# Start addresses of operand parts: split activations and weights placed 0 to 240 bytes into larger tiles

## The chip, the cores and the metric

One core of a Trainium2 chip runs one program. The metric is device time in microseconds of one execution; the median of three runs stands for a kernel.

## The reference

Two stacked blocks on 256 tokens of width 1024, batch 1, in float32. The first block has two layers, each with a gated feed forward, an attention of three kinds of heads (block-sparse, indexed top-64, stick-breaking) and a second gated feed forward, all with a modulated norm. The second block has four layers, each with a mixer (state space, gated linear attention, gated delta rule, state space), attention to a memory of 256 tokens, and a feed forward with a short convolution. Nearly all of the arithmetic is products of activations with weights:

```python
def swiglu(h, w1, w3, w2):                      # first block: 1024 -> 2816 -> 1024, four times
    return (jax.nn.silu(h @ w1) * (h @ w3)) @ w2

def conv_glu_ffn(h, up_w, conv_w, conv_b, down_w):   # second block, four times
    gate, up = jnp.split(h @ up_w, 2, axis=-1)
    gate = causal_dwconv(gate, conv_w) + conv_b
    return (jax.nn.silu(gate) * up) @ down_w
...
        x = x + mix                              # mixer: projections of rmsnorm(x), and an output product
        x = x + memory_cross_attention(rmsnorm_2(x, ln_xattn[i]), rmsnorm_2(mem, ln_mem[i]), ...)
        x = x + conv_glu_ffn(rmsnorm_2(x, ln_ffn[i]), ...)
```

## The kernel before, in words

Activations lie with channels on the 128 partitions and the 256 tokens along them. Every float32 operand of a large product is an exact sum of two parts, a high part (`h` at the end of its name) that ScalarE writes as a copy and a low part (`l`) that another engine writes as the rest (`split`, lines 244 to 247). A product is three matmuls in float32r, high x high, high x low and low x high (`mm3`, line 297), each with a weight load of its own of 128 x 128 and 256 columns of the moving operand; all are issued on line 283.

Weights come from memory in slabs of one MB, 128 partitions x 2048 values (`slab`, line 249): a DMA fills `w` (three places), ScalarE writes `wh`, VectorE `wl` (three places each); with `share` set GpSimd writes a piece of `wl`. An up slab holds 8 chunks of the contraction by 256 columns: one slab is 2 x 8 x 3 = 48 matmuls. A down slab holds 2 chunks by 1024 columns: 48 matmuls too.

Which operand is moving and which the weights: in most products slabs are the weights and the activation moves. In products that leave tokens on the partitions (`proj_half`, `wide_half`) chunks of the activation are the weights and the slab moves. In the profile a matmul is named out<-moving,weights: `up<-hl,wh` moves `hl` over weights from `wh`.

Activation parts: `hh`, `hl` of a norm's output, [128, 8, 256], one place each, made in `norm` (line 550) and `norm_shift` (line 556); `norm_shift` also makes `eh`, `el`, [128, 8, 258], used by the first two slabs of a stage of the first block; `gh`, `gl`, [128, 512], two places each, made in `glu` (line 664) for the input of the down products; `mh`, `ml` of the memory; `oh`, `xoh`, `myh`, `hyh`, `gyh` and their low parts before output products.

`glu` runs over 11 steps of 256 of the 2816 inner columns. A step is two up slabs (96 matmuls) and, one step behind, one down slab (48 matmuls); both blocks use it. The instructions of TensorE stand in the order of the trace within a chain; otherwise a scheduler keeps the order of the program. `gdn_combine` (from line 1888) inverts 128 x 128 triangular matrices of the delta rule, four at a time, and holds a 64 x 64 corner of four of them in `q2` (four places).

Tiles are packed one behind the other along each partition, on multiples of 32 bytes: constants, then `w`, then `wh` and `wl`, then the pool of the norms (`hh`, `hl` and what belongs to them), then what the stage at hand needs. First bytes within a partition in the program before, and what is left of them modulo 256:

| parts | first byte | modulo 256 |
|---|---|---|
| `wh`, three places | 64544, 72736, 80928 | 32 |
| `wl`, three places | 89120, 97312, 105504 | 32 |
| `hh`, `hl` | 120896, 129088 | 64 |
| `eh`, `el` (rows of 1032 bytes) | 212832, 221088 | 96, 160 in the first row, 8 more in each next |
| `gh`, `gl` in the first block | 159968 (and places behind it) | 224 |
| `gh`, `gl` in the second block | 157760 (and places behind it) | 64 |
| `mh`, `ml` in the first stage | 153792, 170176 | 192 |
| `myh`, `hyh`, `xoh`, `xqh`, `xkh`, `xvh` and their low parts | | 64 |
| `oh`, `gyh` and their low parts | | 0 |

Within a tile all of these step by 512 or 1024 bytes from one matmul's operand to the next, but for `eh`, `el`, and but for slabs of the indexer (`wide_half`), whose moving rows are 264 or 320 values long.

Of the kernel before, what the change touches and what calls it, by code (L numbers as in the profile page):

```python
# [9 lines left out]
F32R = mybir.dt.float32r  # L10
# [6 lines left out]
P = 128  # L17
T = 256
# [8 lines left out]
# ---------------------------------------------------------------- layout of small vectors  # L27
# [17 lines left out]
def _consts():  # L45
# [11 lines left out]
        # sums from after a chunk's middle to each token, or negative from after the token to the middle  # L57
# [12 lines left out]
def _prepare(i):  # L70
    """Lays the inputs out: weights as slabs in the order they are used, vectors as columns."""
# [15 lines left out]
    def up(w, order=None):  # L87
        """[.., 1024, n] -> [.., n / 256, 128, 8, 256], column blocks of 128 in the order given."""
        lead, n = w.shape[:-2], w.shape[-1]
        w = w.reshape(-1, KC, P, n // P, P)  # L90
        if order is not None:
            w = w[:, :, :, order]
        nb = w.shape[3]
        w = w.reshape(-1, KC, P, nb // 2, 2 * P).transpose(0, 3, 2, 1, 4)
        return np.ascontiguousarray(w).reshape(*lead, nb // 2, P, KC * 2 * P)

    def down(w):
        """[.., k, 1024] -> [.., k / 256, 128, 2, 1024]."""
        lead, k = w.shape[:-2], w.shape[-2]
        w = w.reshape(-1, k // 256, 2, P, D).transpose(0, 1, 3, 2, 4)  # L100
        return np.ascontiguousarray(w).reshape(*lead, k // 256, P, 2 * D)

    def wide(w):
        """[.., 1024, n] -> [.., 2, 128, 4, n]: halves of the contraction."""
# [4 lines left out]
    def flat(w):  # L109
        """[.., 1024, n] -> [.., 128, 8 * n]."""  # L110
# [62 lines left out]
# ---------------------------------------------------------------- the program  # L173


class Normed:
    """The parts of something to be normed, and each token's factor, once it is worked out."""
# [10 lines left out]
class Net:  # L188
    def __init__(self, tc, a, out):
# [16 lines left out]
        self.n = 0  # L206

    # ---- small helpers

    @contextmanager  # L210
    def phase(self, name):
        """Tiles of a part of the program, given back at its end."""
# [31 lines left out]
    def split(self, src, hi, lo, engine=None):  # L244
        """src as a sum of two parts; returns the two instructions."""
        a = self.nc.scalar.activation(hi, src, AF.Copy)  # L246
        return a, (engine or self.nc.vector).tensor_tensor(lo, src, hi.bitcast(F32), op=OP.subtract)  # L247

    def slab(self, src, n=2048):
        """A slab of weights, as two parts that add up to it exactly."""  # L250
# [6 lines left out]
        hi = self.t([P, 2048], "wh", F32R, pool=self.sp)[:, :n]  # L257
        lo = self.t([P, 2048], "wl", F32R, pool=self.sp)[:, :n]
        m = n // self.pieces
        for k in range(0, n, m):  # L260
# [6 lines left out]
            if self.slabs == 2:  # L267
                # this slab's place is in use until the norm's input is there
                for x, y in zip(s, self.normed):
                    self.after(x, y)  # L270
# [14 lines left out]
    def link(self, ins):  # L285
        """In a chain the tensor engine keeps to the order that is traced."""
# [10 lines left out]
    def mm3(self, out, a, b, start, stop):  # L297
        """out += a.T @ b, both given as exact sums of two parts."""
# [7 lines left out]
    def rsqrt(self, out, src, scale):  # L306
        """out = (src * scale + eps) ** -0.5"""
# [3 lines left out]
    def newton(self, r, src, scale, n):  # L311
        """One step of Newton's for r = (src * scale + eps) ** -0.5"""
# [8 lines left out]
    def after(self, ins, before):  # L321
        """Issues ins behind an earlier instruction of its engine."""
# [7 lines left out]
    def act(self, out, src, func, **k):  # L330
        """An activation of one of the two tables in use: Silu's, or the one with both Ln and Exp. The scalar
        engine takes turns with them as they are traced."""
# [11 lines left out]
    # ---- start  # L344

    def load_cols(self):
        """All vectors but the memory's gains."""
# [33 lines left out]
    def load_consts(self):  # L381
        """Tables, and masks made from them."""
# [11 lines left out]
        # biases: queries on partitions (keys after the query), keys on partitions (keys from the query on)  # L394
# [9 lines left out]
    def start(self, kv):  # L404
        """The first of the memory's keys and values go along with the first modulation."""
# [17 lines left out]
    # ---- modulation  # L423

    def ada_slab(self, l, s):
        """256 columns of layer l's modulation: rows of its weights, over partitions, with silu(c)."""
# [30 lines left out]
    def need(self, l, chunk):  # L457
        """Has columns [chunk * 1024, ..) of layer l's modulation worked out by now."""
# [3 lines left out]
    def mod_cols(self, l, i):  # L462
        """(gain, shift) of the i-th norm of layer l."""
# [19 lines left out]
    # ---- norms  # L483

    def square_sums(self, b, x, s, engine=None, behind=None):
        """Adds the squares of x's pair of chunks b to the sums so far; the last give what is left to add up."""
# [29 lines left out]
    def rstd(self, parts, cols=False, r=None):  # L516
        """Each token's reciprocal root mean square, on all partitions; with cols also over tokens, behind."""
# [12 lines left out]
    def parts_of(self, x, gain, eh, el, sums=True, beside=None):  # L530
        """The parts of x * gain; and the sums of x's squares, but for the last addition."""
# [18 lines left out]
    def norm(self, gain, cols=False):  # L550
        """x normed, as the parts of x * gain, and a factor for each token, which goes to what comes of
        products with them."""
        e = [self.t([P, KC, T], "h" + k, F32R, pool=self.hp) for k in "hl"]
        return Normed(self, e, self.parts_of(self.x, gain, *e), cols)

    def norm_shift(self, gain, shift):
        """x normed and shifted: h, its parts; and for products that need not wait for the root mean
        square: e, x normed, with the parts of the shift behind each chunk."""
# [7 lines left out]
        h = [self.t([P, KC, T], "h" + k, F32R, pool=self.hp) for k in "hl"]  # L566
# [23 lines left out]
    def scale(self, out, ps, r):  # L590
        """out [128, n, T] = products with e, of a bank or a part of it, times r."""
# [5 lines left out]
    def project(self, src, n, tag, bufs=2, bank=None):  # L597
        """Two blocks of a projection of x normed: [128, 2, T]."""
# [7 lines left out]
    # ---- feed forward  # L606
# [5 lines left out]
    def down_step(self, acc, w, j, g, first, last, banks=range(4)):  # L612
        """acc += w[k-chunk j].T @ g"""
# [4 lines left out]
    def down_pair(self, acc, w, g, first, last):  # L618
        """acc += w.T @ g; in the last step one bank after the other is done."""
# [9 lines left out]
    def up_pair(self, out, w, n):  # L629
        """out[j] = w[block j].T @ n; with the first of a norm's products the high parts come first, and then  # L630
        the root mean square. Blocks in halves of a bank, or in two."""
# [32 lines left out]
    def glu(self, part, down, side):  # L664
        """down.T @ part(s, out), in four banks; part works out two blocks of rows at a time."""
# [7 lines left out]
        for s in range(ns):  # L673
            g = self.t([P, 2, T], "g")
            part(s, g)
            gs = [self.t([P, 512], "g" + x, F32R) for x in "hl"]
# [48 lines left out]
    # ---- first block's attention  # L725
# [4 lines left out]
    def proj_tokens_from(self, src, n, h):  # L730
        """h.T @ w for n columns: two banks, tokens on partitions."""
# [5 lines left out]
    def wide_half(self, ps, src, n, h, q):  # L737
        """One half of the contraction of h.T @ w."""
# [8 lines left out]
    def rotate(self, q, t=None):  # L747
        """Rotary embedding of the first 16 dims of each head, in place; q: [128, heads, 64] of one half of
        the tokens, or [128, 2, heads, 64]."""
# [13 lines left out]
    def tok_halves(self, l, n, h, out):  # L763
        """256 columns of a projection, over tokens, in two steps: out [128, 2, 256]."""
# [7 lines left out]
    def qk_halves(self, l, n, k, h, dst):  # L772
        """Norm, gain, rotation and, in a third step, transposition of four heads of queries or keys:
        dst [128, 2, T], queries scaled."""
# [23 lines left out]
    def index_halves(self, l, h, d):  # L798
        """The indexer's projections, in four steps; then their transposition, in two."""
# [35 lines left out]
    def select(self, d):  # L835
        """A bias for each query and key: 0 where the key is among the query's best 64, else -1e30. Five steps
        for the scores, six for the best."""
# [39 lines left out]
    def softmax_head(self, qk, j, v, out, bias=None):  # L877
        """One head, in three steps: qk [128, 4, T] (query pairs, scaled, and key pairs), v [128, 2, 64] tokens,
        out [64, T] in PSUM."""
# [34 lines left out]
    def stick_head(self, q, k, v, out, bank):  # L914
        """Stick-breaking, in three steps: q, k [64, T] (q scaled), v [128, 2, 64] tokens; keys on partitions."""
# [25 lines left out]
    def head_pair(self, head, l, p, oh, ol, wait):  # L941
        """Two heads, one a step behind the other, in four steps; in a fifth the norm of each, gain, and its
        parts."""
# [35 lines left out]
    def attention(self, l):  # L979
        nc, a = self.nc, self.a  # L980
        h, e = self.norm_shift(*self.mod_cols(l, 1))
        # queries and keys of the first stick-breaking heads
# [16 lines left out]
    def qkc_halves(self, l, p, h, q):  # L999
        """Queries and keys of two stick-breaking heads, in two steps: q [128, 2, T]."""  # L1000
# [9 lines left out]
    def attention_heads(self, l, h, qkc):  # L1010
        """Half a slab at a time, with a step of what goes on beside it behind."""
# [78 lines left out]
    # ---- second block: memory attention  # L1090
# [11 lines left out]
    def mem_first(self):  # L1102
        """The memory, and the first slab by turns with it: and what works out the slab's parts, piece by piece."""
        m = self.t([P, KC, T], "mem", bufs=1)
        w = self.t([P, 2048], "w", pool=self.wp)
        self.ready = hi, lo = [self.t([P, 2048], "w" + k, F32R, pool=self.sp) for k in "hl"]
# [6 lines left out]
    def kv(self, i, m=None):  # L1113
        """Keys and values of layer i's memory attention, in steps of a slab."""
# [23 lines left out]
    def proj_pair(self, ps, w, h):  # L1138
        """h.T @ w for 256 columns: the two halves of the tokens in the halves of a bank."""
# [11 lines left out]
    def cross(self, i):  # L1151
# [9 lines left out]
        with self.chained():  # L1161
# [6 lines left out]
            # each head goes through: queries (two steps), scores, turned probabilities, output  # L1168
# [24 lines left out]
    def cross_head(self, hd, kT, v, n, src, oh, ol):  # L1193
        """One head of memory attention, in five steps."""
# [61 lines left out]
    # ---- second block: state space mixer  # L1256

    def softplus(self, out, v, bias, n, tag):
        """out = softplus(v + bias); v, out [n, T]"""
# [8 lines left out]
    def mamba(self, i):  # L1268
        """Half a slab at a time, with what follows on it in between."""
# [3 lines left out]
            "dt": self.t([P, 2, 64], "mdk", bufs=1),  # dt of all heads, and log decays, over tokens  # L1273
# [33 lines left out]
    def mamba_steps(self, ia, n, d):  # L1307
        """dt for all heads, and the log decays' sums: from each token to the end of the first
        half (negative), or from the start of the second."""
# [33 lines left out]
    def out_proj(self, w, gh, gl, n, gate=None):  # L1343
        """x += (w.T @ (gh + gl)) * gate, from 2 * n blocks of rows."""
# [775 lines left out]
```

## Time and profile before

| | |
|---|---|
| runs | 3250.59, 3248.66, 3244.77 us, median 3248.66 |
| span of the profiled execution, first to last instruction | 3242.8 us |
| TensorE matmuls | 25,866, busy 3123.4 us |
| VectorE busy | 2406.3 us |
| ScalarE busy | 1874.0 us |
| GpSimd busy | 614.6 us |
| mean granted clock of TensorE | 0.989 of 2.4 GHz |
| moved by DMA | 624.85 MB, mean 193 GB/s |

The median of the runs is 5.9 us over the span of the profiled execution: the span begins with the first instruction and ends with the last. Busy times of matmuls overlap, since they are pipelined; the time that one matmul takes of TensorE's stream is read from the starts of successive ones, not from its duration.

### The profile page before, as it was taken

The page shows a single profiled execution, that of the slowest core. Times are in us where ns is not written, and L with a number is a line of the kernel's source. Part 1 is how long each engine was busy: PE and PEld are TensorE (multiplying, and loading weights), DVE is VectorE, ACT ScalarE, POOL GpSimd, SP SyncE. Part 2 cuts the span into 40 slices and gives each one's busy share as a digit, 9 for nine tenths or more (in the row PEclk, how much of TensorE's full clock was granted, in tenths as well). Part 3 has the DMA queues.
Part 4 walks back from the last instruction along what each step waited for, and adds up shares of the span by engine and source line. Part 5 has one row for each costly group of instructions (what it writes and reads, how often), then busy time and mean ns, then how long its engine had stood idle before and what let it go on. Part 6 is the DMA issues. An engine that isn't in the chain of part 4 may idle for free. (4 is left out here: it accounts for less than half of the span.)

```text
span 3242.8 us, 63167 instructions
## 1 busy us (share of the span) xinstructions
PE 3123.4 (96%) x25866; PEld 3022.4 (93%) x25866; DVE 2406.3 (74%) x4122; ACT 1874.0 (58%) x3317; POOL 614.6 (19%) x522
## 2 busy tenths in 40 slices
PE   8999999999999999999999999998899999999998
PEld 8999889999988999889999999997799999889998
DVE  6877778777776857887767677688857766887765
ACT  5544566454466546775546655476466545776544
POOL 1100232010032102433001220036422000443100
PEclk9999999999999999999999999999999999999999
DMA  8978436758843655444554445544334555545453
GB/s 286 320 292 312 175 125 216 292 216 298 303 171 120 220 185 187 164 163 170 182 186 155 142 169 173 191 163 157 130 118 156 198 196 186 176 163 184 162 188 118
DMA packets 96754, 624.85 MB, mean 193 GB/s; under 512 B 10640, under 2 KB 14800, under 8 KB 25424
## 3 DMA queue, kind: packets, MB, share of 16 engines
q1 hardware_dynamic: 96464, 620.82, 54.7%
q8 instruction: 203, 3.33, 0.4%
q14 instruction: 87, 0.71, 0.1%
HBM read 607.08 MB, written 13.70 MB: 191 GB/s over the span
## 5 line engine op out<-in xcount | busy, mean ns | idle before, releaser
L246 ACT ACTIVATE wh<-w 128x512 fp32r<-128x512 f32 (+3 forms) x1392 | 1034.7, 788 | 773.7 <-issue 251.0
L247 DVE TENSOR_TENSOR wl<-w,wh 128x512 fp32r<-128x512 f32 (+3 forms) x1195 | 1140.9, 982 | 370.9 <-ACT wh L246 367.3
L283 PE MATMUL up<-hh,wh 128*128 128x256 f32 x4120 | 1158.2, 283 | 6.6 <-DVE gpr L593 6.2
L283 PE MATMUL up<-hh,wl 128*128 128x256 f32 x4120 | 1148.5, 281 | 1.3 <-DVE wl L247 1.0
L283 PE MATMUL up<-hl,wh 128*128 128x256 f32 x4120 | 1133.2, 282 | 4.1 <-DVE hl L247 4.1
L283 PEld LDWEIGHTS up<-hh,wh 128*128 128x128 f32 x4120 | 781.2, 190 | 15.9 <-ACT wh L246 7.0
L283 PEld LDWEIGHTS up<-hh,wl 128*128 128x128 f32 x4120 | 781.1, 190 | 2.6 <-DVE wl L247 2.5
L283 PEld LDWEIGHTS up<-hl,wh 128*128 128x128 f32 x4120 | 771.4, 190 | 7.1 <-DVE hl L247 5.1
L247 POOL TENSOR_TENSOR wl<-w,wh 128x512 fp32r<-128x512 f32 (+1 forms) x197 | 281.6, 1433 | 1395.9 <-ACT wh L246 1272.5
L283 PE MATMUL acc<-gl,wh 128*128 128x256 f32 x1408 | 391.7, 278 | 0.0
L283 PE MATMUL acc<-gh,wl 128*128 128x256 f32 x1408 | 391.5, 278 | 0.0
L283 PE MATMUL acc<-gh,wh 128*128 128x256 f32 x1408 | 391.4, 278 | 0.0
L283 PEld LDWEIGHTS acc<-gh,wl 128*128 128x128 f32 x1408 | 264.9, 188 | 0.0
L283 PEld LDWEIGHTS acc<-gh,wh 128*128 128x128 f32 x1408 | 264.9, 188 | 0.0
L283 PEld LDWEIGHTS acc<-gl,wh 128*128 128x128 f32 x1408 | 264.7, 188 | 0.1
L440 DVE SCALAR_TENSOR_TENSOR w<-w,silu_c 128x512 f32<-128x512 f32 x288 | 190.2, 711 | 55.5 <-DMA w<-ada 55.3
L505 POOL TENSOR_TENSOR nss<-nss,nsq 128x512 f32<-128x512 f32 x38 | 51.4, 1352 | 558.3 <-ACT nsq L492 557.0
L283 PE MATMUL up<-wh,hh 128*128 128x256 f32 (+1 forms) x352 | 106.2, 302 | 5.0 <-ACT hh L246 4.9
L283 PE MATMUL up<-wh,hl 128*128 128x256 f32 (+1 forms) x352 | 101.9, 290 | 1.2 <-DVE hl L247 1.1
L283 PE MATMUL up<-wl,hh 128*128 128x256 f32 (+1 forms) x352 | 101.4, 288 | 0.0
L335 ACT ACT_TABLE_LOAD x71 | 91.1, 1283 | 1.7 <-PEq L2110 0.7
L593 DVE TENSOR_TENSOR fgs<-up,nr 128x512 f32<-128x512 f32 x44 | 30.4, 691 | 80.1 <-PE up L283 80.1
(530 smaller groups left out, 5987.2 us busy)
## 6 DMA issues: line engine op xcount, KB each, us to landing
w<-w SPq DMA_DIRECT2D x132, 1024.0 KB, 5.3
w<-ada SPq DMA_DIRECT2D x72, 1024.0 KB, 5.1
w<-min SPq DMA_DIRECT2D x48, 1024.0 KB, 5.0
w<-fg SPq DMA_DIRECT2D x44, 1024.0 KB, 4.9
w<-fu SPq DMA_DIRECT2D x44, 1024.0 KB, 4.9
w<-fd SPq DMA_DIRECT2D x44, 1024.0 KB, 4.9
w<-gin SPq DMA_DIRECT2D x24, 1024.0 KB, 5.0
w<-xv SPq DMA_DIRECT2D x16, 1024.0 KB, 6.1
```

The source lines that it names most:

```text
L246: a = self.nc.scalar.activation(hi, src, AF.Copy)
L247: return a, (engine or self.nc.vector).tensor_tensor(lo, src, hi.bitcast(F32), op=OP.subtract)
L283: self.link(self.nc.tensor.matmul(out, lhsT=lhsT, rhs=rhs, start=start, stop=stop, skip_group_check=True))
L335: self.loaded = self.nc.scalar.preload_act_table_set(name)
L440: ins = nc.vector.scalar_tensor_tensor(c, c, 1.0, self.silu_c[:, z * 512 : z * 512 + 512], op0=OP.mult, op1=OP.mult, accum_out=sums[:, s % ...
L505: nc.gpsimd.tensor_tensor(s, s, q, op=OP.add)
L593: self.nc.vector.tensor_tensor(out, ps.rearrange("p (b t) -> p b t", b=n), r[:, :T].unsqueeze(1).to_broadcast([P, n, T]), op=OP.mult)
```

## The change

Tiles of the parts of slabs, of norms and of `g` become longer by 128, 224 and 256 bytes, and each new one uses a stretch of the old length within it that begins at another multiple of 16 bytes, the same for the high and the low part. `q2` of `gdn_combine` is no tile of its own but the columns 0 to 63 of `at`, of which it uses the partitions 64 to 127. Comments and docstrings go too. All of the code that changes:

```diff
+        self.count = {"slab": 0, "h": 0, "g": 0}
...
+    def slab_parts(self, n=2048):
+        o = 4 * (self.count["slab"] * 3 % 8)
+        self.count["slab"] += 1
+        return [self.t([P, 2048 + 32], "w" + k, F32R, pool=self.sp)[:, o : o + n] for k in "hl"]
+
+    def h_parts(self):
+        o = 4 * (0, 2, 4, 6, 8, 10, 12, 14, 1, 3, 5, 7, 9, 11, 13, 14)[self.count["h"] % 16]
+        self.count["h"] += 1
+        return [
+            self.t([P, KC * T + 56], "h" + k, F32R, pool=self.hp)[:, o : o + KC * T].rearrange("p (k t) -> p k t", k=KC)
+            for k in "hl"
+        ]
+
+    def g_parts(self):
+        o = 4 * (self.count["g"] * 5 % 16)
+        self.count["g"] += 1
+        return [self.t([P, 512 + 64], "g" + x, F32R)[:, o : o + 512] for x in "hl"]
...
     def slab(self, src, n=2048):
...
-        hi = self.t([P, 2048], "wh", F32R, pool=self.sp)[:, :n]
-        lo = self.t([P, 2048], "wl", F32R, pool=self.sp)[:, :n]
+        hi, lo = self.slab_parts(n)
...
     def norm(self, gain, cols=False):
-        e = [self.t([P, KC, T], "h" + k, F32R, pool=self.hp) for k in "hl"]
+        e = self.h_parts()
...
     def norm_shift(self, gain, shift):
...
-        h = [self.t([P, KC, T], "h" + k, F32R, pool=self.hp) for k in "hl"]
+        h = self.h_parts()
...
     def glu(self, part, down, side):
...
-            gs = [self.t([P, 512], "g" + x, F32R) for x in "hl"]
+            gs = self.g_parts()
...
     def mem_first(self):
...
-        self.ready = hi, lo = [self.t([P, 2048], "w" + k, F32R, pool=self.sp) for k in "hl"]
+        self.ready = hi, lo = self.slab_parts()
...
     def gdn_combine(self, d, q, pool):
...
-        q2 = self.t([P, 4, 64], "gq2", bufs=4, pool=pool)
+        q2 = at[:, :, lo]
```

## Rows read from the trace of the kernel before

**Rows 1.** The page: busy us, share of the span and instructions of each engine.

```profile
PE 3123.4 (96%) x25866; PEld 3022.4 (93%) x25866; DVE 2406.3 (74%) x4122; ACT 1874.0 (58%) x3317; POOL 614.6 (19%) x522
```

**Rows 2.** Span and mean granted clock of the core.

```profile
core 0: 3242.8 us, clock 0.989
```

**Rows 3.** Waits: engine, line, waited for: us in total, times, longest.

```profile
DVE wl L247 <- ACT wh L246: 367.3, 292, 5.0
...
PEld acc L283 <- issue: 19.1, 49, 3.5
```

**Rows 4.** Stretches: length, then busy us (instructions) of each engine.

```profile
core 0: us, PE busy (x) PEld busy (x) DVE busy (x) ACT busy (x) POOL busy (x), PEclk, DMA share, GB/s
176.30:326.00 149.70, 149.70 (x1297) 149.70 (x1296) 116.06 (x217) 65.05 (x74) 0.00 (x0) 1.00 0.83 302
1560.00:1720.00 160.00, 160.00 (x1374) 160.00 (x1373) 109.08 (x136) 78.80 (x97) 0.00 (x0) 1.00 0.56 192
2135.00:2365.00 230.00, 200.03 (x1783) 184.62 (x1782) 196.82 (x340) 148.46 (x315) 114.28 (x115) 0.96 0.42 146
```

**Rows 5.** Chain of waits, in order of time: start us, us, what.

```profile
2564.43 16.80 PE up L283 x144
2581.23 5.60 PE acc L283 x48
...
2789.91 3.39 DVE mbc L2005 x6
```

**Rows 6.** TensorE in order of time, first feed forward: start, us, matmul.

```profile
299.78 0.28 PE L283 MATMUL acc<-gh,wh 128*128 128x256 f32 x1
...
305.24 0.28 PE L283 MATMUL up<-hh,wh 128*128 128x256 f32 x1
...
316.44 0.28 PE L283 MATMUL acc<-gh,wh 128*128 128x256 f32 x1
```

**Rows 7.** TensorE in order of time, the memory's values and keys.

```profile
39.71 0.29 PE L283 MATMUL up<-wh,mh 128*128 128x256 f32 x1
...
62.75 0.28 PE L283 MATMUL up<-mh,wh 128*128 128x256 f32 x1
...
67.21 0.28 PE L283 MATMUL up<-ml,wh 128*128 128x256 f32 x1
...
87.63 0.28 PE L283 MATMUL up<-wh,mh 128*128 128x256 f32 x1
```

**Rows 8.** TensorE in order of time: attention's token products, memory attention's scores.

```profile
1008.00 0.28 PE L283 MATMUL up<-wl,hh 128*128 128x256 f32 x1
...
1010.60 0.28 PE L283 MATMUL up<-wh,hl 128*128 128x256 f32 x1
...
1518.66 0.28 PE L283 MATMUL up<-xkh,xqh 128*128 128x256 f32 x1
...
1519.62 0.28 PE L283 MATMUL up<-xkh,xql 128*128 128x256 f32 x1
```

**Rows 9.** TensorE in order of time: products with `e`, and the indexer's.

```profile
160.46 0.29 PE L283 MATMUL acc<-eh,wh 128*128 128x258 f32 x1
...
171.96 0.29 PE L283 MATMUL up<-hh,wh 128*128 128x256 f32 x1
...
374.13 0.29 PE L283 MATMUL up<-wl,hh 128*128 128x264 f32 x1
...
376.80 0.28 PE L283 MATMUL up<-wh,hl 128*128 128x264 f32 x1
...
383.77 0.31 PE L283 MATMUL acc<-wl,hh 128*128 128x320 f32 x1
...
387.00 0.31 PE L283 MATMUL acc<-wh,hl 128*128 128x320 f32 x1
```

**Rows 10.** Instructions of lines 537 and 1923: duration ns min/median/max.

```profile
L537 ACT ACTIVATE hh<-xT,cols x96: 493/497/516, 1251.1 to 3045.9; 128x256 fp32r<-128x256 f32 x96
L537 ACT ACTIVATE eh<-xT,modA x48: 491/496/513, 127.8 to 1066.7; 128x256 fp32r<-128x256 f32 x48
...
L1923 ACT ACTIVATE gq<-acc x8: 367/378/380, 2350.9 to 2368.6; 64x256 f32<-64x256 f32 x8
```

## The prediction, before the run

> **What bounds the kernel now.** I read the busy times of the engines and the span first. TensorE is busy in 3123.4 of 3242.8 us [rows 1, 2]; a busy TensorE need not be a TensorE at its peak, so the next view is the list of waits. The longest are waits of other engines for each other (VectorE's `wl` for ScalarE's `wh`); the longest of TensorE itself are under 20 us in total [rows 3]. The table of stretches splits the kernel in two kinds [rows 4]. In the feed forward stages (176 to 326 us: one of four of the first block; 1560 to 1720 us: one of four of the second) TensorE is busy in every microsecond. In a mixer (2135 to 2365 us, the delta rule) VectorE is busy for 196.8 of 230 us, and TensorE for 200.0. The chain of waits says the same: in a feed forward stage it is nothing but matmuls, 144 of them in 16.80 us and 48 in 5.60 us; in the last state space mixer it goes through VectorE's work on `mbc` and its like [rows 5].
>
> So over half of the span goes at the pace at which TensorE takes one weight load with one matmul after another, and the change moves exactly the operands of these. The view that matters is therefore the order in time of the matmuls, where the pace of a run is its first start to the next run's start over its count. One step of the first block's feed forward: 96 up products from 305.24 to 316.44 us, 11.20/96 = **116.7 ns**; 48 down products before them, 299.78 to 305.24, 5.46/48 = **113.7 ns** [rows 6]. They have one shape. The second block's down products are made by the same function and go at 5.60/48 = 116.7 ns [rows 5]. What differs between the two is where the operands lie. Call *distance* the byte at which the moving operand starts less that of the weights, modulo 256. By the tables of addresses above it is constant within a run, since every part is a multiple of 256 bytes long and every step within it is one of 512 or 1024:
> - 32 (up products 64 - 32; second block's down products 64 - 32): 116.7 ns
> - 192 (first block's down products, 224 - 32): 113.7 ns
> - 96 (memory's values, weights `m`, 32 - 192): 39.71 to 62.75 us, 23.04/192 = 120.0 ns [rows 7]
> - 160 (memory's keys, 192 - 32): 67.21 to 87.63 us, 20.42/172 = 118.7 ns [rows 7]
> - 224 (token projections of attention, weights `h`, 32 - 64): 1008.00 to 1010.60 us, 2.60/22 = 118.2 ns [rows 8]
> - 0 (scores of memory attention, 64 - 64): 1518.66 to 1519.62 us, 0.96/8 = 120.0 ns [rows 8]
>
> The pace follows the distance, not the function or the stage. Before the change nearly all matmuls have the two best of these six.
>
> **The change part by part.** *Offsets of slabs, h and g.* No instruction is added or removed; three start addresses move. A slab place grows to 8320 bytes, so the three places of `wh` start at 32, 160, 32 and of `wl` at 160, 32, 160 (modulo 256), plus 0, 48, 96, 16, 64, 112, 32, 80 by turns. `hh` and `hl` lie 8416 apart, so they start at 64 and 32, plus a multiple of 16 for each norm. Everything behind them moves by 1216 bytes, 192 modulo 256; `gh` and `gl` get their own turn on top. Worked out over all steps, the distances then fall on all sixteen multiples of 16, evenly within a factor of 1.7, and 38% of the matmuls on the six distances whose pace is known. Within one block of products the distances of the high and the low terms also differ, by 96 or 128.
>
> What pace does such a mixture have? Three answers from rows. (a) The six known, weighted by how often each will occur, average 117.7 ns. (b) The products with the parts `e` are a mixture already: their rows are 1032 bytes long, so the distance moves by 8 with each chunk and goes from 64 to 184; 96 of them take 160.46 to 171.96 us, 11.50/96 = 119.8 ns for 258 columns [rows 9]. (c) The indexer's projections, whose moving rows are 1056 and 1280 bytes long: 374.13 to 376.80 us, 2.67/22 = 121.4 ns for 264 columns, and 383.77 to 387.00 us, 3.23/22 = 146.8 ns for 320 [rows 9]. The last two give 25.4/56 = 0.45 ns a column, so (b) is 118.9 ns and (c) 117.8 ns for 256 columns. I take **118.1 ns**, near (a) and (c). Bounds: were each of the ten unseen distances as good as the best row, the mean would be 0.38 x 117.7 + 0.62 x 113.7 = 115.2; as bad as the worst, 0.38 x 117.7 + 0.62 x 120.0 = 119.1.
>
> The sum, with counts from the code (some 22,700 of TensorE's 25,866 matmuls [rows 1] are of the full form, 128 x 128 weights and 256 columns):
> - First block's feed forward, four stages of 960 up and 528 down products: 960 x 1.4 + 528 x 4.4 = 3.7 us each, **+14.7 us**; TensorE has no gap there, so all of it counts.
> - Second block's feed forward, 4 x 1584 products at 116.7 and 192 of the memory's that go beside them: 6528 x 1.4 = **+9.1 us**, all of it on the path.
> - Mixers and memory attention: 1536 x 2, 768, 1152 and 4 x 384 products at 116.7 ns, 6528 x 1.4 = 9.1 us, less 0.7 for 384 at distance 0. There VectorE and ScalarE end many waits [rows 4, 5], and a slower TensorE fills gaps that are there anyway: I count half, **+4.2 us**. If the cover is gone it is 8.4.
> - Attention's token products are at 118.2 already: 0. The start's 1152 are at 120.0 and 118.7, so they gain 1.4, half of it covered by weights that are still coming: **-0.7 us**.
>
> Sum +27.3 us. *The other engines.* What writes the parts now writes them at other multiples of 16 bytes. `eh`, whose chunks start 8 bytes further each, takes ScalarE 496 ns against 497 for `hh` [rows 10]; VectorE's subtraction is the same kind of unit-step access: 0. *q2 in gdn_combine* goes into a corner of `at` that nothing else reads after it: its copy takes 378 ns [rows 10], eight of them on the same engine in the same order; 0 (if each came late by its own length, 8 x 0.4 = 3 us in a stage with gaps). The four buffers it gives back only make room. The clock was 0.989 of full on average [rows 2]; I take it as unchanged.
>
> **The prediction** is 3242.8 + 27.3 = 3270.1 us for a profiled execution; the runs' median is 5.9 us over the span of this one, so 3248.7 + 27.3 = **3276 us**, 0.8% slower. About 0.2% (6.5 us) is what a measurement of this kernel can tell from no change.
>
> **Rivals.** *Distances that were not seen are the good ones (the other side).* At the bound of 115.2 ns the exposed products (5952 + 6720 in the feed forward, half of 8640 elsewhere: 17,000) go 2.9 ns faster than I take, 27.3 - 49.3 = -22 us: 3227. It decides from a mean of 116.5, that is if the ten unseen average under 0.62 x m + 0.38 x 117.7 = 116.5, m = 115.8. For it: 113.7 exists. Against it: `e` passes over six of the ten and shows 118.9, and (c) 117.8. Chance 0.16, with its middle near 3237.
> *The distance does nothing.* Then paces of 113.7 and 116.7 have another cause and stay: 3249. Against it stand the down products of the two blocks, one function at two paces. Chance 0.10. A rule on the page speaks for this rival: the Trainium skill, "TensorE: Matmul & The Clock Gate", Part 2, step by step, has the weights and the moving operand read through two independent ports, so that loading the next weights takes nothing from the matmul that runs. By that rule the sum is 0. The trace disagrees so far, with 113.7 to 120.0 ns for the same pair of instructions.
> *It is as bad as the worst.* A mean of 119.1 gives 27.3 + 17 = +44 us, 3293, and with nothing covered about 3300. For it: 120.0 at two of six distances, and high and low terms that now differ. It belongs to the slower side; chance 0.12. My own forecast, 3262 to 3290, has 0.62.
>
> **Numbers.** Slower by over 0.2%: 0.62 + 0.12 = 0.74. Same: 0.10. Faster: 0.16. The range goes from 3238 (the middle of the first rival) to 3296 (short of the worst bound): it leaves out some 0.08 below and 0.04 above. The likeliest alone: 3262 to 3290.
>
> **What would show it.** In the order of time, a run of 48 or 96 products keeps one shape but no longer one pace: steps of the first block's feed forward go from 16.66 us to about 17.0, of the second's from 16.80 to 17.0, each by its slab's turn; where a distance of 32 or 192 falls on a run, 116.7 and 113.7 come back, and 120.0 at 96. Busy times of VectorE and ScalarE stay. I am wrong if runs stay at one pace (then it is not the distance), if the mean of the full products is under 116.5 ns, or if mixers grow by more than the feed forward stages (then a wait, not the pace, carries the change).

## The result and the profile after

The kernel after takes **3267.58 us** (median of 3 runs, 3265.21 to 3268.12), against 3248.66 before: a ratio of 1.0059 [1.0045, 1.0073]. It is slower by 18.9 us in the medians and by 23.5 us in the spans of the profiled executions (3242.8 and 3266.3 us). The prediction was 3276 (+27.3), its likeliest case 3262 to 3290. In every later run of this case the span is 1.7 to 1.9 us under the time; so the profile before is of an execution of about 3244.6 us, where the shortest of the three took 3244.77, and the one after of the longest (3268.12), and sums over stages below come out some 5 us above the difference of the medians. Of the 5.9 us that are put down to the ends of the span ahead of the prediction, only some 2 are that.

Span and clock, busy times, and VectorE's wait for ScalarE, from three views of the kernel after; its lines stand 1 to 20 below those of before:

```profile
core 0: 3266.3 us, clock 0.991
```

```profile
PE 3149.1 (96%) x25866; PEld 3050.0 (93%) x25866; DVE 2405.4 (74%) x4122; ACT 1873.5 (57%) x3317; POOL 615.9 (19%) x522
```

```profile
DVE wl L248 <- ACT wh L247: 382.7, 309, 5.0
```

Against [rows 1 to 3]: the counts are the same, the other engines' busy times are within 1.3 us, the clock is no lower (0.991 for 0.989). TensorE alone has more, 25.7 us in its matmuls and 27.6 in its weight loads. The same kinds of stretch as in [rows 4], at their new places:

```profile
178.80:328.50 149.70, 149.70 (x1275) 149.70 (x1274) 115.48 (x215) 64.64 (x74) 0.00 (x0) 1.00 0.82 301
1574.60:1736.30 161.70, 161.70 (x1373) 161.70 (x1373) 108.76 (x135) 78.77 (x98) 0.00 (x0) 1.00 0.55 190
2152.00:2382.00 230.00, 201.74 (x1774) 186.83 (x1772) 194.54 (x337) 147.52 (x313) 114.54 (x115) 0.94 0.41 144
```

In the first line the time is that of [rows 4], at full clock and without a gap, and holds 1275 matmuls where it held 1297: 149.70/1275 = 117.4 ns each for 115.4. Where one matmul follows another, the order in time gives the pace. A step of the first block's feed forward, and what follows it:

```profile
303.74 0.28 PE L303 MATMUL acc<-gh,wh 128*128 128x256 f32 x1
...
309.39 0.28 PE L303 MATMUL up<-hh,wh 128*128 128x256 f32 x1
...
320.70 0.28 PE L303 MATMUL acc<-gh,wh 128*128 128x256 f32 x1
...
326.19 0.28 PE L303 MATMUL up<-hh,wh 128*128 128x256 f32 x1
```

From down product to down product the step has 16.96 us; before it had 16.66 [rows 6]. But the two runs of 48 differ: 5.65/48 = 117.7 ns, then 5.49/48 = 114.4. The chain of waits in the last feed forward stage (start, us, what) shows the same in the second block:

```profile
3107.69 5.69 PE acc L303 x48
3113.38 11.36 PE up L303 x96
3124.74 5.47 PE acc L303 x48
3130.21 11.22 PE up L303 x96
3141.43 5.69 PE acc L303 x48
3147.12 11.40 PE up L303 x96
```

Before, each run of 48 in the second block took 5.60 us [rows 5]; these take 5.47 or 5.69, and 96 take 11.22 to 11.40.

**Where the time went.** The matmuls stand in the same order in both traces (64 have another name, since `q2` is now part of `at`), so a stage's length is read from its first matmul to that of the next stage:

| | before to after, us | difference | predicted |
|---|---|---|---|
| four feed forward stages, first block | 172.0 to 175.2, 175.7 to 179.6, 175.2 to 178.2, 175.8 to 178.3 | +12.6 | +14.7 |
| four feed forward stages, second block | 187.1 to 188.9, 187.2 to 189.0, 232.2 to 235.2, 190.2 to 191.6 | +8.0 | +9.1 |
| mixers | 232.7 to 232.8, 152.3 to 150.8, 317.3 to 318.7, 232.7 to 233.3 | +0.6 | } +4.2 |
| four memory attentions | 61.6 to 61.9, 61.5 to 61.7, 63.0 to 63.6, 61.9 to 62.2 | +1.3 | |
| attention, products with `e` | all eight between -0.3 and +0.3 | -0.8 | 0 |
| start | 153.6 to 155.8 | +2.2 | -0.7 |

The sum is +23.9. The mean pace of all dense full products (128 x 128 weights and 256 columns, start to next start under 128 ns, at full clock) went from 116.75 ns (21,960 of them) to 117.96 (21,862); I had assumed 118.1.

### The profile page after: what moved, and what is told of

The parts are those of the page before. It is cut to its first block, busy times and chain, and to the rows that moved or that the text cites. A ratio compares the mean times of both kernels' runs of the same rounds, so it can differ in the third digit from the quotient of the medians.

```text
span 3266.3 us, 63170 instructions
## 1 busy us (share of the span) xinstructions
PE 3149.1 (96%) x25866; PEld 3050.0 (93%) x25866; DVE 2405.4 (74%) x4122; ACT 1873.5 (57%) x3317; POOL 615.9 (19%) x522
## 5 line engine op out<-in xcount | busy, mean ns | idle before, releaser
L460 DVE SCALAR_TENSOR_TENSOR w<-w,silu_c 128x512 f32<-128x512 f32 x288 | 190.2, 710 | 35.7 <-DMA w<-ada 35.7
```

The source lines that it names most:

```text
L460: ins = nc.vector.scalar_tensor_tensor(c, c, 1.0, self.silu_c[:, z * 512 : z * 512 + 512], op0=OP.mult, op1=OP.mult, accum_out=sums[:, s % ...
```

## The experiments

Two theories were held against each other from the start. **A:** TensorE's pace follows the distance of the operands (modulo 256), and the change costs what the mean over its distances costs. **B:** the distance does nothing; the change costs through its other sides (moved buffers, turning addresses, q2). For runs with mixed distances, the distance is that of a matmul's moving operand to the weights that follow it; this is a choice, and no run shows that it is these weights that count and not the matmul's own. A pace given for a run, here and below, is first start to the next run's start over the count. Times below are against the kernel before on the same chip; a diff shows the lines that matter, against the kernel before or, where it changes `slab_parts`, `h_parts` or `g_parts`, against the kernel after.

**Everything at distance 96, and nothing turns.** The kernel before with tiles that nothing uses ahead of slabs, `h` and `g`. As everywhere below that `padw` stands, q2 has the place that the change gives it.

```diff
+        self.sp.tile([P, 48], F32, name="padw", tag="padw", bufs=1)
+        self.hp.tile([P, 16], F32, name="padh")
...
+        self.t([P, 24], "padg", bufs=1)
...
-        q2 = self.t([P, 4, 64], "gq2", bufs=4, pool=pool)
+        q2 = at[:, :, lo]
```

> Kernel before with one unused tile ahead of the slab parts, one ahead of the norms' parts and one ahead of the first block's feed forward tiles, so that every up and down product and most output products have the distance 96 (moving start less weights' start, modulo 256), nothing turning; q2 in a corner of at, to make room. Theory (the pace follows the distance): the pace of full products is 120.0 ns nearly everywhere; first block's feed forward 4 x (960 x 3.3 + 528 x 6.3) = +26 us, second block's 6528 x 3.3 = +21.5 us, mixers a quarter to a half of 21.5: about 3249 + 53 = 3302, between 3295 and 3310. Rival (it is the turning, or the longer tiles, that cost): nothing turns here, so 3249 within 0.2%.

Measured: 3299.84 us, ratio 1.0154 [1.014, 1.0169]. Its chain in the last feed forward stage:

```profile
3120.86 5.76 PE acc L285 x48
3126.62 11.52 PE up L285 x96
```

That is 120.0 ns a product, the pace that [rows 7] show for this distance, and it costs 2.6 times what the change costs (1.54% for 0.59). All eight feed forward stages go at it. Nothing turns here, so a cost needs no turning; that buffers and q2 have moved, which B could still name, is tested alone further below.

**Everything at distance 192.** The same with tiles of 24, 40 and 24.

> As the run before, with unused tiles of other lengths, so that nearly all full products have the distance 192. Theory: 113.7 ns nearly everywhere; up products of the first block's feed forward 3840 x 3.0 = -11.5 us, second block's feed forward 6528 x 3.0 = -19.6, mixers a third of -19.6, the start half of -3.6: about 3249 - 39 = 3210, between 3200 and 3220. Rival (the cost lies in the turning): 3249 within 0.2%. Rival (113.7 belongs to the down products, not to their distance): 3249, with up products at 116.7.

Measured: 3237.9 us, 0.9962 [0.9951, 0.9974]: faster, but not by what was expected. Two steps in the order of time, of the first and the second feed forward stage:

```profile
288.79 0.28 PE L285 MATMUL acc<-gh,wh 128*128 128x256 f32 x1
...
294.44 0.28 PE L285 MATMUL up<-hh,wh 128*128 128x256 f32 x1
...
305.75 0.28 PE L285 MATMUL acc<-gh,wh 128*128 128x256 f32 x1
```

```profile
604.20 0.28 PE L285 MATMUL up<-hh,wh 128*128 128x256 f32 x1
...
615.08 0.28 PE L285 MATMUL acc<-gh,wh 128*128 128x256 f32 x1
...
620.52 0.28 PE L285 MATMUL up<-hh,wh 128*128 128x256 f32 x1
```

At one distance there are two paces: 11.31/96 = 117.8 ns (and 5.65/48 = 117.7) in the first stage, 10.88/96 = 113.3 (and 5.44/48) in the second. Seven stages keep to their end the one with which they begin; the third of the second block, which also works out the memory's last keys and values, changes several times between the two near its end. Of the eight, three went at 117.8 and the others, in the main, at 113.3. So A in the form "one distance, one pace" fell; a distance has a few steady paces.

**All addresses 96 further.** The kernel before with one unused tile ahead of all others; no distance changes but those of the few products with `e`.

```diff
+        self.cp.tile([P, 24], F32, name="pad")
```

> Kernel before with one unused tile of 96 bytes in front of all others: every tile's start changes by 96, no distance changes but those of the few products with e. Theory (distance alone counts): 3249 within 0.2%, 116.7 and 113.7 ns in the same places. Rival (it is where an operand starts that counts, not how far apart the two start): paces move by 1 ns or more in the feed forward stages, which is 13 us or more either way.

Measured: 3247.51 us, 0.9992 [0.9984, 1.0001]. So moved buffers alone do not cost, and for a shift of 96 bytes it is not where an operand lies that counts but how two of them lie to each other. The same paces in the same places, as expected, came back only in part: in the profiled execution distance 32 showed a second pace, 117.8 in two and most of a third of the second block's stages, 116.7 elsewhere. That made these three stages 4.8 us longer together in an execution of 3250.78 us; the median over eleven runs stands at 0.9992 all the same.

**q2 alone.** Only `q2 = at[:, :, lo]`.

> The kernel before with q2 in a corner of at, and nothing else moved apart from the buffers behind it. By the prediction's term: 0, 3249 us within 0.2%. If the copies come late by their own length, +3 us in the delta rule's stage.

Measured: 3249.3 us, 1.0003 [0.9994, 1.0012]. The term of 0 was right. With moved buffers and q2 tested alone, turning is what is left of B; no run turns addresses while every distance stays, but the kernel whose slabs alone turn (below) has the pace of its distance in nearly every run, the good ones among them.

**High and low parts in step or not.** In the kernel after, the places of `wh` and `wl`, and those of `hh` and `hl`, lie at different remainders of 256, so within one block of products the distances jump. Two kernels part this from the turning itself. The first turns all parts by multiples that leave these jumps at 128. By the weights that follow, all products of a run then have one distance; by its own weights, a product with a low part lies 128 further:

```diff
-        o = 4 * (0, 2, 4, 6, 8, 10, 12, 14, 1, 3, 5, 7, 9, 11, 13, 14)[self.count["h"] % 16]
+        o = 4 * (0, 2, 4, 6, 1, 3, 5, 7)[self.count["h"] % 8]
...
-            self.t([P, KC * T + 56], "h" + k, F32R, pool=self.hp)[:, o : o + KC * T].rearrange("p (k t) -> p k t", k=KC)
+            self.t([P, KC * T + 32], "h" + k, F32R, pool=self.hp)[:, o : o + KC * T].rearrange("p (k t) -> p k t", k=KC)
...
-        o = 4 * (self.count["g"] * 5 % 16)
+        o = 4 * (self.count["g"] * 5 % 12)
...
-        return [self.t([P, 512 + 64], "g" + x, F32R)[:, o : o + 512] for x in "hl"]
+        return [self.t([P, 512 + 48], "g" + x, F32R)[:, o : o + 512] for x in "hl"]
```

> Changed kernel with lengths such that the high and the low terms of a product share one distance (8192 + 128 for slabs and norms, 2048 + 192 for g), still turning over all sixteen multiples of 16. Theory: each run of 48 products has the pace of its own distance, 113.7 at 192, 116.7 at 32, 118.2 at 224, 120 at 96; the mean over all lies within 1 ns of the changed kernel's, and the time between 3255 and 3280. If mixed distances within a product are themselves a cost, this kernel is faster than the changed one by over 0.3%. Rival (distance does nothing): all runs at one pace.

The second lets slabs alone turn, in tiles of 8192 + 256 bytes, so that high and low parts have one remainder:

```diff
-        o = 4 * (self.count["slab"] * 3 % 8)
+        o = 4 * (self.count["slab"] * 5 % 16)
...
-        return [self.t([P, 2048 + 32], "w" + k, F32R, pool=self.sp)[:, o : o + n] for k in "hl"]
+        return [self.t([P, 2048 + 64], "w" + k, F32R, pool=self.sp)[:, o : o + n] for k in "hl"]
```

> Slab parts alone turn, over sixteen multiples of 16, in tiles of 8192 + 256, so that high and low part and all three places have one remainder; norms' parts and g lie as in the kernel before; one buffer less of a small tile in the delta rule, to make room. In the run with the same turns for high and low the runs did not keep to their distance's pace. Theory A (because high and low parts lay 128 apart, and a matmul meets both): here runs of 48 go at 116.7 at distance 32, 118.3 at 224, 120 at 96, 113.4 or 117.8 at 192, and the paces spread over more than 5 ns. Theory B (a run of 48 is too short for a pace of its own): all sixteen within 117 to 119 ns as in the changed kernel. Both: time between 3255 and 3280, since the mean stays near 118.

Measured: 3269.47 us, 1.0058 [1.0045, 1.0071], with a mean of 117.95 ns; and 3272.68, 1.0075 [1.006, 1.0091], with 118.23. In the first, runs did not have their distance's pace: 48 down products at distance 192 took 5.65 us (from 584.02) and 5.70 (from 652.16), and over the whole runs of 48 in the feed forward stages the means by distance lie between 117.4 and 118.9 ns, single runs between 116.6 and 119.8. So the weights that follow are not all that counts. In the second they did. Its chain in the last stage, where the down products' distances are 0, 16, 32, 48 and 64 in turn (by the table of addresses):

```profile
3093.80 5.76 PE acc L303 x48
...
3111.02 5.76 PE acc L303 x48
...
3127.96 5.60 PE acc L303 x48
...
3144.94 5.60 PE acc L303 x48
...
3161.97 5.66 PE acc L303 x48
```

So 120.0, 120.0, 116.7, 116.7, 117.9 ns, each kept for its run. The other stages agree: of 246 whole runs of 48 without a gap, over all sixteen distances, 242 lie within 0.5 ns of the median of their distance, and these medians go from 113.5 to 120.0. At 192 it has 113.4 to 113.8 in all fourteen runs, at 96 119.7 to 120.0 in all fifteen. So with high and low parts in step each distance has its own pace even for 48 products, and with a step of 128 between them the fastest (192) and the slowest (0, 96, 144) have lost it. The step is no cost beside that: both kernels stand near the kernel after (1.0058 and 1.0075 for 1.0059), and the one with its paces intact is no faster.

**One distance for a whole stage.** Slabs keep still; each feed forward stage has one distance of its own.

```diff
+        o = (60, 0, 8, 20, 0, 36, 0, 0, 4, 0, 0, 12, 0, 0, 24, 0, 0, 28)[self.count["h"]]
...
+        o = (20, 32, 44, 60, 4, 12, 24, 28)[self.count["g"] // 11]
```

> Nothing turns within a stage: slabs still, each of the eight feed forward stages with one distance for all its products (first block 16, 64, 112, 176; second 48, 80, 128, 144), high and low alike. Theory (a lasting distance locks the two streams into a steady pace, one or two for each distance): every stage shows one steady pace to 0.3 ns over its length, between 113.3 and 120.0 ns, and they differ from distance to distance; 64 at 113.4 or 117.8. Rival (steady paces belong to multiples of 32 alone): paces of 16, 48, 80, 112, 144, 176 wander.

> As the run before with distances 208, 240, 16, 64 in the first block's feed forward stages and 208, 240, 112, 176 in the second's. Theory: a steady pace in each stage; where a distance comes again (16, 64, 112, 176 across the two runs) it has the same pace or the other of two, as 192 had 113.3 and 117.8. Rival (pace by distance alone, one each): the same pace again to 0.3 ns.

Measured (the second has other lists): 3265.71 and 3267.38 us, one run each. Paces by distance: 16: 116.7 and 118.7; 48: 118.3; 64: 117.8 in both; 80: 120.0; 112: 113.3 and 113.6; 128: 118.6, and 120.0 from the middle of its stage on; 144: 118.7; 176: 119.3 in both; 208: 119.2 and 240: 117.1, each in both of its stages. So multiples of 16 have steady paces too; all stages but that at 128 kept theirs. Only 112 was as good as 192, though in runs of 48 of the kernel with turning slabs it went at 119.7 nearly each time. It, too, has more than one pace.

**Up products at 192, down products at 32.** Unused tiles of 24, 40 and 48, and 24 in the second block's feed forward.

> Unused tiles such that up products have distance 192 and down products 32 in all eight feed forward stages, the kernel before's first-block alternation turned round. There, runs at 192 entered from a run at 32 had 113.7 in all stages, while a whole stage at 192 had 113.3 or 117.8. Theory (the state at 192 is set by what comes before, and 32 ahead of it leads to the low one): up products at 113.7 in all eight stages; first block's feed forward 4 x (960 x -3.0 + 528 x 3.0) = -5 us, second block's 4224 x -3.0 = -13, mixers and start -6: about 3225, steadier than the kernel with 192 alone. Rival (the state is drawn at random at each entry): paces mixed within a stage, 3235 to 3245.

Measured: 3233.02 us, 0.9947 [0.9935, 0.996]. The first feed forward stage from its beginning:

```profile
177.12 0.28 PE L285 MATMUL up<-hh,wh 128*128 128x256 f32 x1
...
188.43 0.28 PE L285 MATMUL acc<-gh,wh 128*128 128x256 f32 x1
...
194.03 0.28 PE L285 MATMUL up<-hh,wh 128*128 128x256 f32 x1
...
204.93 0.28 PE L285 MATMUL acc<-gh,wh 128*128 128x256 f32 x1
```

The first 96 at distance 192 take 11.31 us, 117.8 ns: exactly what the kernel with everything at 192 kept through this stage. Then come 48 at distance 32 (5.60, 116.7 ns), and the next 96 at 192 take 10.90: 113.5 ns. Four other stages did the same. But one was at 113.3 from its beginning, and in the second and third stage of the first block the 96 behind the first run at 32 still went at 117.8 (from 555.06 and from 745.75 us); those behind the second had 113.5. From there on the low pace stayed, but for one run at 117.8 at the end of the first stage, behind a gap in TensorE's work. So the state is not a matter of the distance alone: what ran before has a part in it, but one run at 32 does not decide it each time. The time came out between the two expectations, 8 us above the theory's 3225 and 2 under the rival's 3235 to 3245.

**Distance 112.** With 20 for all `h` of the feed forward and the second block, and 44 and 20 for `g` (first and second block); then the same `h` with `g` at distance 32 (24, 0) or 192 (0, 40):

```diff
+        o = (20, 0, 20, 20, 0, 20, 20, 20, 20, 20, 20, 20, 20, 20, 20, 20, 20, 20)[self.count["h"]]
...
+        o = (44, 20)[self.count["g"] // 44]
```

> The kernel before with activation parts shifted so that nearly all products run at distance 112, high and low parts alike; slabs as before; q2 in a corner of at. Theory (a distance has a few steady paces, and the long stages at 112 ran at 113.4 and 113.65): against the kernel before, 3840 up products x -3.2, 2112 first-block down products x -0.2, 6336 of the second block x -3.2, together -33 us, and up to -10 in the mixers: 3206 to 3216 us. Rival (the state is set by what comes before, and 112 has the pace of 119.7 too, as in the runs of 48): +3.0 for up and second block, +6 for the first block's down products: 3285 to 3300 us. A mixture by stages lies between; the trace then shows whole stages at either.

> As the run at 112, but the down products at distance 32. If a run of 48 at 32 puts the next run in its low state, as it did for 192, up products go at 113.5 in all eight stages and down products at 116.7: 8064 x -3.2 + 2112 x +3.0 = -19.5 us, and up to -10 in the mixers: 3219 to 3229 us. If 112 then takes 119.7: 8064 x +3.0 + 6.3 = +31 us, 3279 or more.

> As the run at 112, but the down products at distance 192. If both keep their low states: 8064 x -3.2 and 2112 second-block down products x -3.0 = -32 us, and up to -10 in the mixers: 3207 to 3217 us. If 192 takes its 117.8 and 112 its 119.7: 8064 x +3.0, 2112 x +4.1, 2112 x +1.1 = +35 us: 3284 us. A step that alternates shows which state follows which.

Measured: 3221.62 us, 0.9914 [0.99, 0.9927]; 3232.86, 0.995 [0.9937, 0.9963]; 3221.63, 0.9911 [0.9896, 0.9927]. The first and the last are the fastest kernels of this study, some 46 us below the kernel after. All at 112, the chain in the last stage:

```profile
3051.98 5.44 PE acc L303 x48
3057.42 10.88 PE up L303 x96
```

113.3 ns for both, at a granted clock of 1.00: with 2.4 GHz that is 272 clocks for 256 columns, and the 120.0 ns at distance 96 are 288. The other seven stages have 113.3 too, but for single runs of up to 114.5 and for gaps in the first. Yet each of the three came out 4 to 6 us above the upper end of what A expected. Of the kernel at 112 the second block's stages gave 4.9, 4.7, 4.5 and 5.1 us (19.2; expected 20.3) and three of the first block's 3.3, 2.5 and 3.3. Its first stage got 1.2 us *longer* though its products were faster by 3.1 in sum. The stretch between 236 and 258 us (columns as in [rows 4]), and ScalarE's wait for slabs in it:

```profile
236.00:258.00 22.00, 20.92 (x180) 20.33 (x178) 16.59 (x36) 9.87 (x12) 0.00 (x0) 1.00 0.82 304
```

```profile
ACT wh L247 <- DMA w<-w: 10.6, 3, 9.0
```

ScalarE waits 10.6 us for slabs that come no sooner than before, and TensorE stands idle for 1.1 of 22.0 us; between 318 and 336 us it does so again, for 1.2 us. And of the 10 us in the mixers nothing arrived, though their dense products were faster by 8.5 us in sum: 232.7, 152.3, 317.3 and 232.7 us became 234.1, 151.7, 318.7 and 233.4. In the other two kernels 112 did not take 119.7 ns either: behind 48 at 32 or 192 its 96 up products had 113.3 to 114.9.

## Why the prediction was right, and where it was not

The sum said +27.3 us; the medians moved by 18.9, and the stages of the two profiled executions by 23.9. Every large term was somewhat too big, and the mechanism behind them, TensorE's pace by the operands' distance, is what the experiments show.

- **The pace of the mixture, 118.1 ns.** Measured: 117.96. That is the term that carries the rest, and the reason that it gives holds in this: the time follows the distance (distance 96 for all: 1.0154; distance 112 for all: 0.9914; all addresses moved together: 0.9992). How the mean comes about is another matter, below. Of the three answers, (a), the mean over known distances, and (c), the indexer's rows, were nearest.
- **First block's feed forward, +14.7.** +12.6, that is 2.1 ns a product over 5952 instead of 2.5: some of its down products kept a good pace (114.4 ns from 320.70), where the sum has them all at 118.1. (The sum takes 6528 products for the second block, the rivals 6720; the difference is worth 0.6 us there.)
- **Second block's, +9.1.** +8.0.
- **Mixers and memory attention, +4.2.** +1.9. Their dense products got slower by 6.8 us in sum, so 28% of it showed where I had counted half. The kernel at 112 says the same from the other side: products faster by 8.5 us there bring nothing. There VectorE is busy for 194.5 of 230 us, and the chain goes through its work [rows 5].
- **Start, -0.7.** +2.2, and not to be put down to the change: in the kernel with q2 alone, which issues the same start from the same distances as before, the first `hh` product starts at 175.81 us, against 171.96 [rows 9]; in the kernel after at 173.74; over all experiments it lies between 172.48 and 177.38. Its dense products did get faster, by 1.3 us.
- **"116.7 and 113.7 come back ... and 120.0 at 96": the step that failed.** They came back in part. Over the runs of 48 in the feed forward stages, those with two products of three at 192 range from 113.3 to 118.9 ns, those at 32 from 117.0 to 119.0, those at 96 from 117.8 to 119.4; by single product the means there are 117.2, 117.9 and 119.2. I had weighted each distance by its own pace as though a product knew only one distance. The two kernels with parts in step and out of step show what I had named and not used, that high and low terms differ: out of step by 128, a run is pulled toward 118. The mean survived this since that is also about where the mean of the distances lies (118.23 with parts in step, 117.95 without). Nothing in the prediction gives a reason for that, so as far as the runs show it is luck.
- **The rival that distances not seen are the good ones** had no case in this change: the mean stayed over its point of 116.5. But one of them, 112, is good when it is held for a whole stage, so its premise was not empty.
- **The rival that the distance does nothing** is excluded by the experiments. The rule set beside it, the two independent ports of the Trainium skill ("TensorE: Matmul & The Clock Gate", Part 2, step by step), would give 0 for each of them; the runs gave 1.0154 for 96 and 0.9914 for 112 with the same instructions in the same number, so for this pair of operands the measurement decides against it.

**What stays open.** Why a distance has two steady paces is not settled. At 192 the low one follows a run at 32 as a rule, with two exceptions, and it also comes without one: in the second stage of the kernel with all at 192, and in all fourteen runs of the kernel with turning slabs, where the run before is at 16, 112 or 176. What in the entry decides, and why 112 keeps 119.7 in short runs between others and 113.3 in long ones, no run tells apart. Nor does any run show whether a matmul's own weights count or those that follow, or what the two operands contend for, if that is what they do.

## What to carry to other kernels

Where a stage is a dense row of weight loads and matmuls, divide its time by their number and compare this pace between stages: two paces for one shape are a reason to ask where the operands lie, and moving tiles by a few dozen bytes is worth a measurement (here from 1.0154 to 0.9911 of the time, with no instruction more or less). Hold one good distance through a stage, with high and low parts at the same remainder, rather than spread the distances: spreading gives the mean, and the mean was worse than what the kernel had. Count such a gain only in stages where TensorE has no gap; in the mixers dense products faster by 8.5 us in sum brought nothing.

## What was not expected of the hardware

- At one distance there are two steady paces, held over hundreds of matmuls: 113.3 and 117.8 ns at 192, 116.7 and 117.8 at 32, 116.7 and 118.7 at 16, 118.6 and 120.0 at 128. At 112 it is 113.3 over whole stages and 119.7 in runs of 48 between other distances.
- Which one a run takes is not a matter of the distance alone: 117.8 for the first 96 of a stage at 192, 113.5 from the next on, with 48 at distance 32 between, in five of eight stages; in two more the change came one step later.
- It is the difference of two start addresses that counts: 96 bytes more for all tiles gave 0.9992 [0.9984, 1.0001].
- Parts that are out of step by 128 take a distance its pace: means of 117.4 to 118.9 ns over sixteen distances, where parts in step give 113.5 to 120.0.
- A mean pace better by 2.0 ns (114.77 for 116.75) brought 26 us, one worse by 2.9 (119.65) cost 50: 13 us a nanosecond on the way down, 17 on the way up. Late slabs and the mixers took back part of the gain, as the kernel at 112 shows.
